# Twenty weight slots in place of seventeen, fp32 expert bias and a new order of the works in a transformer layer on one core

## The chip, the cores and the metric

The kernel runs on 1 core of a Trainium2 chip, as one launch. The metric is the device time of that core in microseconds (us), the median of 3 runs. All tensors are fp32 in HBM; there is one execution per run.

## The reference, cut to what matters

One layer over 256 latent tokens (d_model 1024) and 256 context tokens: a mixer of two attention branches (8 heads of GQA and 8 heads of MLA), then a mixture of 32 experts, of which each token takes 4. Both are modulated by rows of an `ada` projection of the conditioning vector: shift, scale and gate, `g1` for the mixer, `g2` for the experts.

```
h  = rms_norm(x)*(1 + scale1) + shift1 ; hc the same for the context
y  = sig(gate_a) * (gqa(h, hc) @ w_o_gqa) + sig(gate_b) * (mla(h, hc) @ w_o_mla)
x  = x + g1 * (y @ w_out)
h2 = rms_norm(x)*(1 + scale2) + shift2
p  = softmax-gated top 4 of 32 of (h2 @ router)
x  = x + g2 * sum_e p_e * (swiglu_clamped(h2 @ w1[e] + b1[e]) @ w2[e] + b2[e])
```

`w1` has 32 x 1024 x 2048 elements and `w2` 32 x 1024 x 1024: 12 MB for each expert, 384 MB in all. Everything before the experts reads about 80 MB.

## The kernel before, in words

**Two parts.** Up to some 407 us of the profiled execution lies the mixer, with the router at its end; then come the 32 experts. Every weight is read once, whether or not many tokens use it.

**The mixer** is cut into works, each a generator that gives up control after a few instructions: `T` (tokens transposed), `r, c, f, h, l, k` (first projection), `q, g` (queries, gates), `p, a, b` (MLA), `S, P, V` (scores, probabilities, values of 16 heads), `wa, wb` (branch projections, two chunks of 512 columns each), `o` (output projection, `out_chunk`), `rest` (the 16 later rows of `ada`, `ada_rest`, each a matmul group at L249 and then columns at L260 or a broadcast at L269), `bi` (preparation of the expert bias, `bias1`) and `x` (the residual read again). The string `PLAN` lists the works in the order in which their steps are issued; `needs` has what must be finished first. Dense products are made at near fp32 accuracy as three matmuls of split operands (L145 to L147), whose weights are split on ACT (L110) and on POOL or DVE (L112).

**Expert weights** come as 1 MB loads, 8 of `w1` (L968) and 4 of `w2` (L1002) for each expert, into a ring of 17 slots in SBUF (`RING`, `wx`). Most slots hold other things during the mixer: keys and values of attention (`e`, `m`), gates (`g`), the merged branches (`y`), or the streaming buffer `w` of the mixer's own weights; `n0` to `n3` lie in memory that all the mixer's pools give back at its end. A load can be issued as soon as its slot's last reader is done.

**What sets the order.** All loads of weights are issued by SyncE (SP), in order: a load that waits for its slot holds back all that follow it. For the experts, `keep_order` fixes each engine's order as written. In the mixer a scheduler places the loads by where the program's text has them.

**One expert**: up to 64 tokens. `gather` (L925 ff., once for each pair of experts) builds a one-hot matrix on DVE (L932), scaled on POOL (L934), gathers with 16 matmuls (L940) and evicts (L946, L948). `up` starts its two banks with the bias (4 bf16 matmuls at L964, from a three-way bf16 split of `b1` in 96 rows) and adds 32 matmuls (L972). `swiglu` is a chain on DVE and ACT; `turned` transposes (L163) and copies (L994); `down` has 16 matmuls (L1007) and an eviction (L1013); `scatter` (L1022, L1023), for each pair, adds into the residual, and writes the output (L1025) after the last. Between `up` and `turned` of an expert, steps of a scatter or a gather stand on PE. The last expert has none there. `b2` is loaded and added by `bias2` in the third expert.

Of the kernel before, what the change touches and what calls it, by code (L numbers as in the profile page):

```python
# [24 lines left out]
T0*3 l0 T0 f0 f1 h0 h1 T0 k0 f2 r1 l1 h2 c1 k1 f3 k2 c2 T1 h3 r5 f4 k3 T1 bi h4 tab T0 f5 r4 bi T1 l4 c0 r2 bi  # L25
T1 r0 f6 l3 r3 T1 l2 k4 k5 h6 T1 r7 c3 f7 k6 k7 end q0 bi T1 bi q0 l5 q0 T0 c7 l6 kv*2 h7 ss bi c5 kv*2 q0 bi
r6 q0 kv bi q0 q1 h5 kv mp q1 bi q0 q1 bi q0 bi q1 mp bi l7 q0 c6 q0 q1 q0 q1 end g0 q1*3 g0*2 bi g0 q1 c4
g0*4 g1 q1 g1 g0 g1 S0 g1 S2 g1*2 P0 S0 g1 g2 rest*2 P1 g2 g1 mp V0 rest*2 g1 g2*2 S2 g2 S4 g2 S3 g2*3 rest g3
rest S1 g3 rest P2 S3 S4 V2 S1 g3*2 rest g2 P3 g3*2 V3 g3 a0 g3 P4 rest S5*2 rest a0 V4 a0 rest g3 rest*3 a0
# [5 lines left out]
wb1 rest o0*4 wb1*2 o0 o1 o0*2 rest wb1 o0 o1*8 x o1*3
"""
SLOTS = ("e0", "e1", "e2", "e3", "m0", "m1", "g0", "g1", "y0", "y1")

RING = ("e0", "e1", "e2", "e3", "m0", "m1", "g0") + ("w",) * NW + ("y0", "y1", "n0", "n1", "n2", "n3", "g1")
# [9 lines left out]
class Layer:  # L49
# [174 lines left out]
    def silu(self):  # L224
# [6 lines left out]
        self.cs = self.k2([128, 8, 32], "cs")  # L231
# [3 lines left out]
        self.bsc = self.k2([128, 2, 8], "bsc")  # L235
# [476 lines left out]
    def ada_rest(self):  # L712
        nc, I = self.nc, self.I
# [14 lines left out]
        last(15, ev)  # L728

    def out_chunk(self, c):  # L730
# [38 lines left out]
    def mixer(self):  # L769
# [7 lines left out]
        def gates(c):  # L777
            if c // 2 not in self.ga:
# [40 lines left out]
    def route(self):  # L819
# [9 lines left out]
        self.xn = self.q([128, 2, D], "xn", 1)  # L829
# [54 lines left out]
    def bias1(self):  # L884

        nc = self.nc
        v = nc.vector
# [3 lines left out]
        f = f.rearrange("p h c -> p (h c)")  # L891
        self.b1 = self.k([96, 2 * D], "b1", BF)
        self.sel = self.k([96, NE], "bsel", BF)
        v.tensor_copy(self.sel, self.ck[:96, K_E32:K_E32 + NE])
        for c in range(4):
            cs = slice(c * 512, (c + 1) * 512)
            v.tensor_copy(self.b1[:, cs], f[:, cs])
            yield
            for lo in (32, 64):
                r = slice(lo, lo + 32)  # L900
# [24 lines left out]
    def gather(self, e0):  # L925

        nc = self.nc
        xg = self.xg = self.q([128, 8, 2, 64], "xg")
        oh, og = self.a([128, 2, 2, 64]), self.a([128, 2, 2, 64])
        sh = [128, 2, 64]  # L930
        for t in range(2):
            nc.vector.tensor_tensor(oh[:, t], self.ck[:, K_I64:K_I64 + 64].unsqueeze(1).broadcast_to(sh),  # L932
                                    self.rp[:, t, e0:e0 + 2].unsqueeze(2).broadcast_to(sh), op=OP.is_equal)
            nc.gpsimd.tensor_tensor(og[:, t], oh[:, t], self.gm[:, t, e0:e0 + 2].unsqueeze(2).broadcast_to(sh), op=OP.mult)  # L934
        yield
        for kk in range(8):
# [12 lines left out]
            yield
        b = self.bank("x", [128, T])  # L950
# [6 lines left out]
    def up(self, e, xg):  # L957
# [276 lines left out]
```

## Time and profile before

| | |
|---|---|
| median of 3 runs | 1351.97 us (the two near it 1351.41 and 1351.97; one far off, 3543.51) |
| the profiled execution | 1351.25 us, of which its span is 1349.5 us |
| PE busy in the span | 1217.8 us (90%), mean granted clock 0.971 |
| DVE, ACT, POOL busy | 457.3, 288.8, 162.8 us |
| HBM read, written | 465.82 MB, 1.05 MB; mean 346 GB/s |
| chain that ended last | PE 51%, DMA 37%, DVE 8% |

The slices of the profile read in two halves. In the first 12 of 40 slices (up to about 405 us) the moved bytes swing between 32 and 348 GB/s, while PE is at 0.6 to 0.9; in all later ones but the last, 399 to 422 GB/s are moved and the DMA engines are at 0.9 or above. Clock figures are shares of full speed; a slice at 0.5 would be the lower of two levels throughout.

### The profile page before, as it was taken

How to read it: one execution, taken by the hardware profiler on the slowest of the kernel's cores; microseconds unless marked ns; L12 is line 12 of the kernel's file. 1: busy time of each engine (PE TensorE's matmuls, PEld its weight loads, DVE VectorE, ACT ScalarE, POOL GpSimd, SP SyncE). 2: the span in 40 equal slices, each digit the busy share in tenths (PEclk: the TensorE clock that was granted, in tenths of full speed). 3: DMA queues.
4: the chain of work that ended last, by engine and by line, in shares of the span. 5: the costliest groups of instructions: out<-in, count | busy, mean ns of one | idle time of the engine just before them, and what ended most of it. 6: DMA issues, size and time to landing. Idle time of an engine off the chain costs nothing.

```text
span 1349.5 us, 15322 instructions
## 1 busy us (share of the span) xinstructions
PE 1217.8 (90%) x6031; PEld 605.2 (45%) x6031; DVE 457.3 (34%) x968; ACT 288.8 (21%) x626; POOL 162.8 (12%) x181
## 2 busy tenths in 40 slices
PE   6979999899988999999999989889898898989896
PEld 5667775667863333433344332333333242433331
DVE  5777447785341132221221211212121112212112
ACT  3356666666430001100010000100000000100000
POOL 2645421233520000000000000000000000000000
PEclk9989999999989989999999999999999999999998
DMA  8614646403879999999999999999999999999994
GB/s 348 238 62 182 228 140 222 145 32 126 327 306 399 408 413 421 421 422 421 421 420 421 421 421 421 421 422 420 422 421 422 421 421 421 422 421 420 422 422 188
DMA packets 67227, 467.91 MB, mean 347 GB/s; under 512 B 7632, under 2 KB 7760, under 8 KB 11760
## 3 DMA queue, kind: packets, MB, share of 16 engines
q1 hardware_dynamic: 67152, 466.89, 85.2%
q8 instruction: 49, 0.80, 0.2%
q14 instruction: 26, 0.21, 0.0%
HBM read 465.82 MB, written 1.05 MB: 346 GB/s over the span
## 4 chain that ended last, share of the span: by engine, by line
PE 51%; DMA 37%; DVE 8%; ACT 2%; issue 1%; POOL 1%; SPq 0%; DVEq 0%; ACTq 0%; POOLq 0%
PE bs L972 15%; PE bx L1007 9%; DMA e<-in_w_dram 9%; DMA n<-in_w_dram 7%; DMA w<-in_w_dram 6%; DMA g<-in_w_dram 5%; DMA m<-in_w_dram 4%; DMA y<-in_w_dram 4%; PE bacc L145 3%; PE bacc L147 3%; PE bacc L146 3%; PE bacc L940 2%; PE bx L163 2%; PE bt L940 2%; PE bx L249 2%; PE bt L163 1%
## 5 line engine op out<-in xcount | busy, mean ns | idle before, releaser
L981 ACT ACTIVATE a<-a 128x512 f32<-128x512 f32 x32 | 20.1, 629 | 716.5 <-DVE a L980 716.5
L980 DVE TENSOR_SCALAR a<-bs 128x512 f32<-128x512 f32 x32 | 22.1, 692 | 435.2 <-PE bs L972 435.2
L972 PE MATMUL bs<-e,xg 128*64 128x512 f32 x504 | 114.8, 596 | 8.1 <-DMA e<-in_w_dram 8.1
L112 POOL TENSOR_TENSOR wl<-w,wh 128x512 fp32r<-128x512 f32 (+1 forms) x81 | 105.3, 1309 | 126.2 <-ACT wh L110 106.9
L934 POOL TENSOR_TENSOR c<-c,gm 128x128 f32<-128x128 f32 x32 | 12.1, 399 | 870.6 <-DVE c L932 854.8
L972 PE MATMUL bs<-n,xg 128*64 128x512 f32 x472 | 108.0, 596 | 9.7 <-DMA n<-in_w_dram 9.7
L1013 DVE TENSOR_TENSOR y<-bx,g 64x512 f32<-64x512 f32 x64 | 44.0, 688 | 207.3 <-PE bx L1007 206.6
L972 PE MATMUL bs<-w,xg 128*64 128x512 f32 x360 | 82.8, 596 | 6.8 <-DMA w<-in_w_dram 6.8
L940 PE MATMUL bacc<-c,xn 128*128 128x128 f32 x256 | 42.9, 337 | 38.6 <-DVE c L932 37.8
L110 ACT CAST wh<-w 128x512 fp32r<-128x512 f32 (+1 forms) x108 | 65.2, 612 | 42.4 <-PE bacc L147 32.8
L972 PEld LDWEIGHTS bs<-e,xg 128*64 128x64 f32 x504 | 34.8, 136 | 82.1 <-issue 58.9
L972 PEld LDWEIGHTS bs<-n,xg 128*64 128x64 f32 x472 | 32.5, 136 | 79.7 <-issue 56.9
L940 PEld LDWEIGHTS bacc<-c,xn 128*128 128x128 f32 x256 | 39.3, 242 | 51.9 <-DVE c L932 51.0
L972 PE MATMUL bs<-m,xg 128*64 128x512 f32 x248 | 57.0, 595 | 3.8 <-DMA m<-in_w_dram 3.8
L972 PE MATMUL bs<-g,xg 128*64 128x512 f32 x240 | 57.1, 596 | 3.8 <-DMA g<-in_w_dram 3.8
L972 PE MATMUL bs<-y,xg 128*64 128x512 f32 x224 | 52.1, 597 | 4.8 <-DMA y<-in_w_dram 4.8
L1007 PE MATMUL bx<-n,a 128*64 128x512 f32 x232 | 54.1, 611 | 0.0
L1007 PE MATMUL bx<-e,a 128*64 128x512 f32 x232 | 52.3, 595 | 0.0
L972 PEld LDWEIGHTS bs<-w,xg 128*64 128x64 f32 x360 | 24.9, 136 | 59.8 <-issue 44.4
L946 DVE TENSOR_SCALAR xg<-bt,A,B 128x128 f32<-128x128 f32 x64 | 21.9, 405 | 79.7 <-PE bt L940 74.3
L1007 PE MATMUL bx<-w,a 128*64 128x512 f32 x192 | 46.2, 626 | 0.7 <-ACT a L994 0.7
L948 ACT ACTIVATE xg<-bacc,B,A 128x128 f32<-128x128 f32 x64 | 24.1, 456 | 73.2 <-PE bacc L940 73.2
(351 smaller groups left out, 1966.6 us busy)
## 6 DMA issues: line engine op xcount, KB each, us to landing
e<-in_w_dram SPq DMA_DIRECT2D x92, 1024.0 KB, 19.8
n<-in_w_dram SPq DMA_DIRECT2D x88, 1024.0 KB, 19.8
w<-in_w_dram SPq DMA_DIRECT2D x69, 1024.0 KB, 19.8
m<-in_w_dram SPq DMA_DIRECT2D x46, 1024.0 KB, 19.8
g<-in_w_dram SPq DMA_DIRECT2D x45, 1024.0 KB, 19.8
y<-in_w_dram SPq DMA_DIRECT2D x44, 1024.0 KB, 19.8
w<-in_ada_dram SPq DMA_DIRECT2D x24, 1024.0 KB, 5.6
w<-in_wga_dram SPq DMA_DIRECT2D x8, 1024.0 KB, 4.8
```

The source lines that it names most:

```text
L110: self.nc.scalar.copy(h, src)
L112: eng.tensor_sub(l, src, h.bitcast(F32))
L145: mm(o, lh, rh, start=start, stop=False, **kw)
L146: mm(o, lh, rl, start=False, stop=False, **kw)
L147: mm(o, ll, rh, start=False, stop=stop, **kw)
L163: self.nc.tensor.transpose(o, i, self.ident)
L249: nc.tensor.matmul(b[j:j + 32, :256], self.cs[:, kk], u[:, kk], start=kk < 4, stop=kk >= 4, tile_position=(0, j))
L940: nc.tensor.matmul(b[:, kk % 4], self.xn[:, t, kk * 128:(kk + 1) * 128], oh[:, t], start=t == 0, stop=t == 1)
L948: nc.scalar.activation(xg[:, k], b[:, i], AF.Identity, bias=c, scale=a)
L972: mm(b[64 * j:64 * j + 64], xg[:, k, e % 2], w[:, lo:lo + 512], start=False, stop=k == 7, tile_position=(0, 64 * j))
L1007: nc.tensor.matmul(b[64 * j:64 * j + 64], lh, w[:, i, j * 512:(j + 1) * 512], start=f == 0, stop=f == 7, tile_position=(0, 64 * j))
L1013: nc.vector.tensor_mul(y[r:r + 64, cs], b[q], self.g2[q, cs])
```

## The change

- **Slots.** `RING` has 20 slots: `z0`, `z1` and `r0` are new. Pools are laid out anew: `ws` and a new pool `r` stand on the right side, `x2T` goes through work tiles, `xg` and `y` have one buffer each, and the attention's own pools (`h`, `k2`) are closed when the last values are done (`after_attention`), so `n0` to `n3` exist before the mixer ends. `dynamic_dma_scratch_size=1024` makes a scratch area in SBUF smaller.
- **Early loads.** Three new works issue 14 expert loads from the plan: `EZ` (2, into `z0, z1`), `EA` (after `V15`: 8, into `e` and `n`), `EG` (after `wb1`: 4, into `m` and `g`). The other 6 of the ring (`w` three times, `y0, y1, r0`) follow as before.
- **Expert bias.** `bias1` with its bf16 split is gone. `biases` loads `b1` (two halves of 32 rows) and `b2` into one fp32 tile; `up` starts with 4 plain fp32 matmuls over 32 rows. `b2` is no longer loaded among the experts.
- **Works.** `rest` keeps 12 rows of `ada`; the 4 of `g2` are the work `late`, placed near the mixer's end. `PLAN` is another order throughout.
- **Gather** evicts in quarters, and makes the scaled one-hot and its transposes after the matmuls; those of the first gather stand behind `up(0)`.
- **The end.** The scatter of the last pair is made in two parts of 64 rows: that of expert 30 between `up(31)` and `turned`, that of expert 31 at the end.

```diff
-RING = ("e0", ..., "m0", "m1", "g0") + ("w",) * NW + ("y0", "y1", "n0", "n1", "n2", "n3", "g1")
+LATER = ("n0", "n1", "n2", "n3")
+RING = ("z0", "z1", "e0", "e1", "e2", "e3") + LATER + ("m0", "m1", "g0", "g1") + ("w",) * NW + ("y0", "y1", "r0")
...
+    def expert_part(self):
+        e, i = divmod(self.nx, 12)
+        src = self.I["w1"][e, i * 128:i * 128 + 128] if i < 8 else self.I["w2"][e, i * 256 - 2048:i * 256 - 1792]
+        w = self.wx([128, 2 * D] if i < 8 else [128, 2, D])
+        self.nc.sync.dma_start(w, src if i < 8 else src.rearrange("(p j) d -> p j d", j=2))
+        return w
+    def weights(self):
+        return self.ahead.pop(0) if self.ahead else self.expert_part()
+    def after_attention(self):
+        self.attention.close()
+        self.open(self.ctx, "q", 1)
+        for slot in LATER:
+            self.q([128, 2, D], slot, 1)
+        self.q([128, D], "xg", 1)
+        yield from self.ahead_of_time(8)
...
-    def ada_rest(self):
+    def ada_rest(self, lo, hi):
...
-        for i in range(16):
+        for i in range(lo, hi):
...
+        w = self.works = {..., "rest": self.ada_rest(0, 12), "late": self.ada_rest(12, 16), ...}
+        need = {..., "late": ["rest"], "EA": ["EZ", "V15"], "EG": ["EA", "wb1"]}
+        w.update(EZ=self.ahead_of_time(2), EA=self.after_attention(), EG=self.ahead_of_time(4))
...
-    def bias1(self):
-        f = self.s("x", [96, 2, D])
-        for j in range(3):
-            nc.sync.dma_start(f[32 * j:32 * j + 32], self.I["b1"].rearrange("e (h c) -> e h c", h=2))
-        ...
-        for c in range(4):
-            v.tensor_copy(self.b1[:, cs], f[:, cs])
-            for lo in (32, 64):
-                for part in range(lo // 32):
-                    v.tensor_sub(f[r, cs], f[r, cs], self.b1[r, cs])
-                    v.tensor_copy(self.b1[r, cs], f[r, cs])
+    def biases(self):
+        self.b12 = self.k([128, D], "b12")
+        for j in range(2):
+            nc.sync.dma_start(self.b12[64 + 32 * j:96 + 32 * j], self.I["b1"][:, j * D:j * D + D])
+        nc.sync.dma_start(self.b12[0:NE], self.I["b2"])
...
     def up(self, e, xg):
-                mm(b[64 * j:64 * j + 64], self.sel[:, e:e + 1].broadcast_to([96, 64]), self.b1[:, lo:lo + 512],
-                   start=True, stop=False, tile_position=(0, 64 * j))
+                r = slice(64 + 32 * n, 96 + 32 * n)
+                mm(b[64 * j:64 * j + 64], self.ck[r, K_E32 + e:K_E32 + e + 1].broadcast_to([32, 64]),
+                   self.b12[r, j * 512:j * 512 + 512], start=True, stop=False, tile_position=(64 + 32 * n, 64 * j))
-            w = self.wx([128, 2 * D])
-            nc.sync.dma_start(w, self.I["w1"][e, k * 128:(k + 1) * 128])
+            w = self.weights()
...
-    def scatter(self, G, y, last):
+    def scatter(self, G, y, last, r=slice(0, 128)):
-                nc.tensor.matmul(b, G[:, t * 128:(t + 1) * 128], y[:, cs], start=True, stop=True)
+                nc.tensor.matmul(b, G[r, t * 128:(t + 1) * 128], y[r, cs], start=True, stop=True)
...
     def experts(self):
-                side = self.gather(e + 1) if e + 1 < NE else iter(())
+                side = self.scatter(self.G, y, False, slice(0, 64))
...
-        for _ in self.scatter(*shown, True):
+        for _ in self.scatter(self.G, y, True, slice(64, 128)):
```

(The plan itself, of which one line would tell nothing, is shown by the orders below.)

**SP around the last branch projection.** Each row is one load; `wob` and `wout` are the mixer's last weights, `in_w` is an expert's, and the letter before the arrow is the slot. Before:

```order
L450 DMA w_3539<-in_wob_dram 128x2048
L760 DMA x_3675<-in_x_dram 128x1024 x2
L450 DMA w_3576<-in_wob_dram 128x2048
L450 DMA w_3633<-in_wob_dram 128x2048
L450 DMA w_3700<-in_wob_dram 128x2048
L968 DMA e_988_4117<-in_w_dram 128x2048
L968 DMA e_989_4123<-in_w_dram 128x2048
L450 DMA w_3776<-in_wout_dram 128x2048
L968 DMA e_990_4129<-in_w_dram 128x2048
L450 DMA w_3806<-in_wout_dram 128x2048
L968 DMA e_991_4135<-in_w_dram 128x2048
L450 DMA w_3862<-in_wout_dram 128x2048
```

And now, the same place, up to the last `wob` and the first `wout`:

```order
L477 DMA w_3510<-in_wob_dram 128x2048
L104 DMA e_851_3474<-in_w_dram 128x2048
L477 DMA w_3570<-in_wob_dram 128x2048
L104 DMA e_843_3453<-in_w_dram 128x2048
L104 DMA e_852_3476<-in_w_dram 128x2048
L104 DMA n_853_3478<-in_w_dram 128x2048
L104 DMA n_854_3480<-in_w_dram 128x2048
L104 DMA e_842_3451<-in_w_dram 128x2048
L104 DMA n_855_3482<-in_w_dram 128x2048
L104 DMA n_869_3565<-in_w_dram 128x2048
L477 DMA w_3637<-in_wob_dram 128x2048
L477 DMA w_3713<-in_wout_dram 128x2048
```

These follow it on the same queue, up to the last two loads of `ada`:

```order
L272 DMA w_3743<-in_ada_dram 128x2048
L477 DMA w_3756<-in_wout_dram 128x2048
L104 DMA m_937_3829<-in_w_dram 128x2048
L477 DMA w_3806<-in_wout_dram 128x2048
L272 DMA w_3816<-in_ada_dram 128x2048
L104 DMA m_938_3831<-in_w_dram 128x2048
L104 DMA g_939_3833<-in_w_dram 128x2048
L104 DMA g_943_3854<-in_w_dram 128x2048
L477 DMA w_3899<-in_wout_dram 128x2048
L272 DMA w_3921<-in_ada_dram 128x2048
L272 DMA w_3951<-in_ada_dram 128x2048
```

Eight expert loads of this stretch now stand ahead of the last `wob`, and four more ahead of the last `wout` and the last two `ada` loads; before, none stood ahead of a `wob`, and five ahead of the last `wout` (two rows behind the last one shown).

**DVE near the end of the first projection.** `x_523` is the fp32 bias, `b_136` its bf16 parts; L299 makes a modulated token block and L141 its low part, for which PE waits. Before:

```order
L299 TENSOR_SCALAR c_684<-m_26_104,A_30_114,B_31_115 128x256
L902 TENSOR_TENSOR x_523<-x_523,b_136_527 32x512 x2
L903 CAST b_136_527<-x_523 32x512 x2
L897 CAST b_136_527<-x_523 96x512
L902 TENSOR_TENSOR x_523<-x_523,b_136_527 32x512 x2
L141 TENSOR_TENSOR c_687<-c_684,c_686 128x256
L903 CAST b_136_527<-x_523 32x512 x2
L112 TENSOR_TENSOR wl_715<-h_174_692,wh_714 128x512
L902 TENSOR_TENSOR x_523<-x_523,b_136_527 32x512
L262 TENSOR_SCALAR B_31_115<-bx_705,cols_89 128x2
L263 TENSOR_SCALAR A_30_114<-bx_705,bsc_111,cols_89 128x2
L903 CAST b_136_527<-x_523 32x512
```

And now, where L326 is what L299 was, and L168 what L141 was:

```order
L326 TENSOR_SCALAR c_630<-e_27_105,A_32_116,B_33_117 128x256
L168 TENSOR_TENSOR e_35_119<-c_630,e_34_118 128x256
L326 TENSOR_SCALAR c_663<-m_28_106,A_32_116,B_33_117 128x256
L168 TENSOR_TENSOR c_666<-c_663,c_665 128x256
L326 TENSOR_SCALAR c_693<-m_28_106,A_32_116,B_33_117 128x256
L289 TENSOR_SCALAR B_33_117<-bx_699,cols_91 128x2
L168 TENSOR_TENSOR c_696<-c_693,c_695 128x256
L290 TENSOR_SCALAR A_32_116<-bx_699,bsc_113,cols_91 128x2
L139 TENSOR_TENSOR wl_709<-h_169_650,wh_708 128x512
L326 TENSOR_SCALAR c_712<-e_27_105,A_32_116,B_33_117 128x256
L326 TENSOR_SCALAR c_740<-m_28_106,A_32_116,B_33_117 128x256
```

The subtractions and casts of the bias stood between the modulations; none is left.

**PE at the end of the program.** `w` of the last `up` (L972 before, L984 now), the transposes of `turned` (L163, L190), `down` (L1007, L1018) and the scatter (L1022, L1033). Before:

```order
L972 MATMUL bs_7880<-m_1807_7928,xg_7699 64x512 x2
L972 MATMUL bs_7881<-m_1807_7928,xg_7699 64x512 x2
L163 MATMUL bx_7942<-ck_90,a_7936 128x128 x4
L1007 MATMUL bx_7949<-g_1814_7950,a_7947 64x512 x4
L1007 MATMUL bx_7949<-w_7956,a_7947 64x512 x4
L1007 MATMUL bx_7949<-w_7962,a_7947 64x512 x4
L1007 MATMUL bx_7949<-w_7968,a_7947 64x512 x4
L1022 MATMUL bacc_7976<-y_7833,c_7742 128x512
L1022 MATMUL bacc_7980<-y_7833,c_7742 128x512
L1022 MATMUL bt_7984<-y_7833,c_7742 128x512
L1022 MATMUL bt_7988<-y_7833,c_7742 128x512
```

And now:

```order
L984 MATMUL bs_7892<-r_1847_7940,xg_7709 64x512 x2
L984 MATMUL bs_7893<-r_1847_7940,xg_7709 64x512 x2
L1033 MATMUL bacc_7954<-y_7845,c_7754 128x512
L1033 MATMUL bacc_7957<-y_7845,c_7754 128x512
L1033 MATMUL bt_7960<-y_7845,c_7754 128x512
L1033 MATMUL bt_7963<-y_7845,c_7754 128x512
L190 MATMUL bx_7966<-ck_92,a_7948 128x128 x4
L1018 MATMUL bx_7973<-z_1858_7974,a_7971 64x512 x4
L1018 MATMUL bx_7973<-z_1859_7980,a_7971 64x512 x4
L1018 MATMUL bx_7973<-e_1860_7986,a_7971 64x512 x4
L1018 MATMUL bx_7973<-e_1861_7992,a_7971 64x512 x4
L1033 MATMUL bacc_8000<-y_7845,c_7754 128x512
```

Four scatter matmuls stand between `up` and `turned` now; the four at the end, of which the last row here is the first, stay as many as before.

## Rows read from the trace of the kernel before

**Rows 1.** Windows: stretch, its us; PE, PEld, DVE, ACT, POOL busy; clock, DMA, GB/s.

```profile
46.00:75.00 29.00, 23.70 (x133) 17.99 (x132) 27.40 (x52) 7.32 (x18) 18.31 (x30) 0.93 0.42 158
75.00:87.00 12.00, 12.00 (x51) 9.70 (x50) 4.95 (x10) 10.19 (x29) 8.96 (x9) 0.89 0.26 88
180.00:293.00 113.00, 100.61 (x618) 68.87 (x617) 80.72 (x222) 72.91 (x175) 23.84 (x23) 0.95 0.42 147
293.00:390.00 97.00, 96.51 (x481) 76.17 (x480) 48.56 (x92) 49.67 (x94) 43.85 (x34) 1.00 0.57 216
390.00:407.00 17.00, 10.73 (x70) 9.69 (x70) 9.29 (x40) 5.34 (x13) 0.76 (x2) 0.70 0.95 388
440.00:800.00 360.00, 339.91 (x1618) 138.82 (x1616) 85.44 (x151) 28.48 (x61) 5.29 (x14) 0.97 1.01 419
1325.00:1330.00 5.00, 2.58 (x8) 1.15 (x10) 1.41 (x3) 0.58 (x1) 0.00 (x0) 0.70 0.59 244
1330.00:1340.00 10.00, 9.21 (x33) 2.90 (x30) 1.38 (x2) 0.00 (x0) 0.00 (x0) 0.81 0.04 16
```

**Rows 2.** Chain in the experts, 440 to 800: start us, us, engine, tile, line.

```profile
549.66 13.76 PE bs L972 x64
...
593.18 1.91 PE bacc L1022 x4
595.10 0.86 PE bt L1022 x2
...
604.73 13.76 PE bs L972 x64
```

**Rows 3.** Chain at the end, 1310 to 1350.

```profile
1302.50 19.80 DMA m<-in_w_dram
...
1322.35 1.96 PE bs L972 x8
...
1326.69 1.00 PE bx L163 x4
...
1328.41 9.76 PE bx L1007 x32
```

**Rows 4.** Timeline of SP's queue, 300 to 412: start us, us, line, load.

```profile
395.04 0.33 SPq L968 DMA_DIRECT2D g<-in_w_dram  x1
408.81 2.04 SPq L968 DMA_DIRECT2D e<-in_w_dram  x2
```

**Rows 5.** Timeline of PE, 389 to 412: start us, busy us, line, operation, [idle before].

```profile
389.82 0.40 PE L147 MATMUL bacc<-wh,y 128*128 128x512 f32 x1
...
398.78 0.19 PE L847 MATMUL bx<-maskb,ub 128*128 128x32 bf16 x1 [3.77 <-DVE maskb L844]
...
399.84 3.75 PE L940 MATMUL bacc<-c,xn 128*128 128x128 f32 x16 [0.77 <-DVE g L862]
...
406.12 0.38 PE L163 MATMUL bx<-ck,c 128*128 128x128 f32 x2
406.43 0.63 PE L964 MATMUL bs<-b,bsel 96*64 96x512 bf16 x4
406.88 5.32 PE L972 MATMUL bs<-e,xg 128*64 128x512 f32 x24
```

**Rows 6.** Chain from 46 to 75 us, shares by line.

```profile
by line: DVE x L902 28.0%; DVE b L903 21.5%; issue 7.1%; DVE c L299 6.4%; DVE b L897 5.9%; DVE wl L112 4.9%; DVE e L141 4.5%; DVE c L141 3.2%; ACT c L140 2.6%; PE bs L147 2.4%; DVE B L262 2.2%; DVE A L263 2.0%; PE bt L145 1.7%; PE bt L146 1
```

**Rows 7.** Timeline of PE, 222 to 240: one row of `ada` and its broadcast.

```profile
229.23 1.07 PE L249 MATMUL bx<-w,cs 128*32 128x256 f32 x16
230.23 0.70 PE L269 MATMUL bx<-c,ck 128*128 128x256 f32 x2
```

**Rows 8.** DMA issues of the page: line, engine, count, KB each, us to landing.

```profile
e<-in_w_dram SPq DMA_DIRECT2D x92, 1024.0 KB, 19.8
```

**Rows 9.** DMA issues from 290 to 412 us.

```profile
w<-in_wob_dram SPq DMA_DIRECT2D x4, 1024.0 KB, 4.9
w<-in_wout_dram SPq DMA_DIRECT2D x4, 1024.0 KB, 6.4
```

More of the change, by code (lines that the diff above doesn't have):

```diff
@@ L24 @@
 PLAN = """
[L25 to L29, printed above, removed]
@@ L35 @@
[L35 to L39 removed]
+bi T0*2 l0 f0 f1 h0 T0 h1 T0 k0 f2 r1 l1 h2 r0 k1 f3 k2 c2 T1 h3 r5 f4 k3 T1 h4 tab f5 r4 l4 c0 T1 r2 T0*2
+T1*2 r3 T1 l2 f6 l3 EZ k4 r7 k5 h6 f7 k6 c1 k7 end q0 T1 q0 c5 kv*2 l5 q0 T0 c7 l6 h7 ss c3 EZ*2 kv q0 r6 q0
+kv q0 kv q1 h5 q1 kv q0 q1*3 g0 l7 q0 q1 q0 c6 q0 q1*2 g0 q0 end q1 g0*2 q1 g1 q1 c4 g0*4 g1 mp g0 g1 mp S0 g1
@@ L61, in open @@
         kw.setdefault("reuse_waits", "tile")
+        if name in ("ws", "r"):
+            kw["side"] = "right"
         self.pools[name] = ctx.enter_context(self.tc.tile_pool(name=f"{name}{self.n}", bufs=bufs, **kw))
@@ L93, in wx, with ahead_of_time @@
             return self.w(shape, dt)
-        return self.tile("q" if slot[0] == "n" else "s", shape, dt, slot, 1)
+        return self.tile({"n": "q", "r": "r"}.get(slot[0], "s"), shape, dt, slot, 1)
+    def expert_part(self):
[6 more added lines that the diff above has]
+        return self.ahead.pop(0) if self.ahead else self.expert_part()
+    def ahead_of_time(self, n):
+        for _ in range(n):
+            self.ahead.append(self.expert_part())
+            yield
+    def after_attention(self):
[5 more added lines that the diff above has]
+        yield from self.ahead_of_time(8)
     def k(self, shape, tag, dt=F32):
@@ L727, in ada_rest @@
             ev = new
-        last(15, ev)
+        last(hi - 1, ev)
     def out_chunk(self, c):
@@ L748, in out_chunk @@
                 self.transpose(b[:, j], self.x[:, t, c * 512 + j * 128:c * 512 + (j + 1) * 128])
-            nc.vector.tensor_mul(self.x2T[:, ks, ts], b, self.A2[:, ks, 0:1].broadcast_to([128, 4, 128]))
-            for k in range(4 * c, 4 * c + 4):
-                nc.tensor.matmul(self.logits[:, t], self.x2T[:, k, ts], self.rw[:, k], start=k == 0 and t == 0, stop=k == 7,
+            x2T = self.a([128, 4, 128])
+            nc.vector.tensor_mul(x2T, b, self.A2[:, ks, 0:1].broadcast_to([128, 4, 128]))
+            for j in range(4):
+                k = 4 * c + j
+                nc.tensor.matmul(self.logits[:, t], x2T[:, j], self.rw[:, k], start=k == 0 and t == 0, stop=k == 7,
                                  skip_group_check=True)
@@ L919, in bias2 @@
                 b = self.bank("acc")
-                nc.tensor.matmul(b, gT[:, t * 128:(t + 1) * 128], b2[:, cs], start=True, stop=True)
+                nc.tensor.matmul(b, gT[:, t * 128:(t + 1) * 128], self.b12[0:NE, cs], start=True, stop=True)
                 z = self.a([128, 512])
@@ L1031, in experts @@
         first = len(self.nc.cur_bb.bb.instructions)
-        for _ in self.gather(0):
-            pass
-        side, shown = iter(()), None
+        gather = self.gather(0)
+        for _ in range(9):
+            next(gather)
+        shown = None
         for e in range(NE):
-            xg = self.xg
-            act = self.swiglu(*self.up(e, xg), 512)
+            act = self.swiglu(*self.up(e, self.xg), 512)
             if e % 2 == 0:
-                side = self.scatter(*shown, False) if shown else iter(())
-                y = self.q([128, D], "y")
+                side = self.scatter(*shown, False) if shown else gather
+                y = self.tile("r", [128, D], F32, "y", 1)
+            elif e + 1 < NE:
                 shown = self.G, y
+                side = self.gather(e + 1)
             else:
-                side = self.gather(e + 1) if e + 1 < NE else iter(())
+                side = self.scatter(self.G, y, False, slice(0, 64))
             for _ in range(7 if e % 2 else 3):
@@ L1081, in overflow @@
             v.memset(one, 1.0)
-            h2 = [self.q([128, 4, T], "xg") for _ in range(2)]
+            h2 = [self.q([128, 4, T], "xg", 1), self.tile("r", [128, 4, T], F32, "y", 1)]
             self.normed_T(h2)
-            ge = self.k([128, 2], "goe")
+            ge = self.q([128, 2], "goe", 1)
             with tc.For_i(0, NE, 1) as i:
@@ L1142, in build @@
     def build(self):
-        self.loaded, self.nsplit, self.nx = {}, 0, 0
+        self.loaded, self.ahead, self.nsplit, self.nx = {}, [], 0, 0
         self.open(self.ctx, "w", 1)
@@ L1147, in build @@
             self.s(slot, [128, 2, D])
+        self.attention = ExitStack()
         with ExitStack() as pre:
-            for p in ("h", "k2", "ws"):
-                self.open(pre, p, 1)
+            self.open(pre, "ws", 1)
+            for p in ("k2", "h"):
+                self.open(self.attention, p, 1)
             self.setup()
```

81 lines of the change are left out of this document (35 added, 46 removed).

## The prediction

> **What bounds the kernel now.** I read the stages first [rows 1]. There are two limits. Among the experts (440 to 800 us is typical) the DMA share is 1.01 and 419 GB/s are moved, so a 1 MB load (1.0486 million bytes) costs 2.50 us; eight are in flight, and 8 x 2.50 is the 19.80 us of one load's latency [rows 8]. PE is the quicker there: two experts start 604.73 − 549.66 = 55.07 us apart while loads are still ahead of it [rows 2], or 27.5 us for one, against 12 x 2.50 = 30.0 us for an expert's loads. So the experts end by DMA, and the chain at the end shows it: a load of 19.80 us, issued at 1302.50, releases the last matmuls of `up` at 1322.35 [rows 3].
>
> The mixer is another matter. In 293 to 390 PE is busy 96.51 of 97 us: PE is the limit, and DMA has room (0.57). In 46 to 75 PE is busy only 23.70 of 29 us while DVE is at 27.40, and the shares of the chain there name the bias split: L902 28.0%, L903 21.5%, L897 5.9% [rows 6].
>
> The join: the last output matmul starts at 389.82, PE then waits for the router, and `up(0)` starts at 406.88 [rows 5]. The first load into a used slot is issued 1.93 us later, at 408.81 [rows 4]. By then 17 of 384 loads are done or under way. The last `w1` load is the 380th; so 363 loads and `b2` take 408.81 to 1322.35 = 913.5 us, 2.52 each. From 1322.35 to the end of the span are 27.15 us. The time is therefore **start of `up(0)` + 1.93 + loads left x 2.50 + tail**, and each part of the change is priced by which of these it moves. The sum is made against the profiled execution, 1351.25 us (span 1349.5 and 1.75 around it), which is 0.7 us below the median of the runs.
>
> **The change, part by part.**
>
> *Bias split removed.* 28 DVE instructions leave the chain. Its share, 55.4% of 29 = 16.1 us, is the most that can come back [rows 6]; none comes back if other DVE or ACT work ends the same waits. I take what PE loses there: 29 − 23.70 = 5.3 us idle, 0.07 x 29 = 2.0 us of clock, and 0.11 x 12 = 1.3 us of clock in the 12 us behind it [rows 1]: **−8.6**, between 0 and −16.1. The change's order on DVE has nothing in their place, so no new wait is due there.
>
> *Four rows of `ada` moved to the end.* A row with its broadcast takes 1.0 us (229.23 to 230.23) and half of 0.70 [rows 7]: 1.35 us, 5.4 for four. They go where PE has no idle time [rows 1], so all of it counts: +5.4. They leave a stretch in which PE is busy 100.61 of 113 us, so 0.89 of it comes back: −4.8 (0 if they filled waits, −5.4 if not). Net **+0.6**, between 0 and +5.4.
>
> *SP's queue.* Eight expert loads now stand ahead of the last `wob` and twelve ahead of the last `wout`; before, none and five. The mixer's loads landed in 4.9 and 6.4 us with the DMA about half used [rows 9]. With an expert load under way, each mixer load lands up to 2.50 later. Most were issued well ahead of their use, so I take **+1.5**, between 0 and +4; the larger loss is a rival.
>
> *Start of `up(0)`.* Four bf16 matmuls (0.45 us from 406.43 to 406.88) become four fp32 ones; a matmul of `up` takes 13.76/64 x 2 = 0.43 [rows 2], so 1.7 us in a row. The transposes of the gather go behind `up(0)` (0.3 us, 406.12 to 406.43 [rows 5]). Net **+1.0**, between 0 (two row tiles at once) and +1.3. The quarter evictions I cost at nothing: they run beside the 16 gather matmuls.
>
> *Three more slots.* 360 loads in place of 363 remain behind `up(0)`, if all 20 have landed: **−7.5**, between 0 and −7.5. That they do: of the six that come last, `y0, y1, r0` must follow the last output matmul, and between it and `up(0)` lie 17.06 us [rows 5], room for 6.8 loads of 2.50. *`b2`* (128 KB, an eighth of a load) leaves the stream: **−0.3**.
>
> *Each expert.* The bias adds 1.3 us to PE's 27.5: 28.8, still below 30.0, so it costs nothing while loads set the pace; the cover is 1.2 us an expert, and each us beyond costs 32. Single buffers of `xg` and `y` are read before they are written again in PE's order, and cost nothing under the same cover.
>
> *The end.* Four scatter matmuls go into the gap that PE has between 1324.31 and 1326.69. By an earlier scatter (1.91 and twice 0.86 [rows 2]) they take 3.6 us, the gap is 2.4: +1.2. Behind the gap the clock falls to 0.70 and 0.81 [rows 1], and `down` takes 9.76 us [rows 3]; 0.30 x 5 + 0.19 x 10 = 3.4 us are lost to the lower level. Whether a filled gap keeps it up no row shows; half is −1.7. Net **−0.5**, between +1.2 and −2.2.
>
> The Trainium skill ("TensorE: Matmul & The Clock Gate", "HAM oscillation") says that idle gaps between bursts of matmuls put TensorE back to its low clock. By that all 3.4 us would return, and the sum would be 1.7 lower.
>
> *The new order of the rest.* Works of equal content change places; no row prices that. In 180 to 293 PE loses 12.4 us idle and 0.05 x 113 = 5.7 of clock [rows 1], 18 in all; both the gain and a loss of that kind are possible. I take **0**, ±6 within the forecast.
>
> Sum: −8.6 + 0.6 + 1.5 + 1.0 − 7.5 − 0.3 − 0.5 = −13.8, or **1337.5 us**.
>
> **Rivals.**
> 1. *The order recovers the 180 to 293 stretch too.* For: the removed DVE work, four `ada` rows less, and nothing else is the limit there (DVE 80.72, ACT 72.91 of 113). Against: its waits are short chains between engines, and only their order is new. All 18: 1319.5. Chance 0.19.
> 2. *Slower: the loads hold up SP.* In the order now, an `e` and two `n` loads stand directly ahead of the last `wob`, and one of them waits until keys or values of the last heads are read; all behind it wait with it. PE would then stand idle in the stretch that has no slack now. Price: nine mixer loads (the last `wob`, four `wout`, four `ada`), each late by one expert load of 2.50: 22.5 us, 1360. It decides once these stalls exceed the 13.8 of the gain. For: the stretch is PE's entirely. Against: five `e` and `m` loads already stood among the `wout` loads, without a gap on PE. Chance 0.12.
> 3. *The slots bring nothing*, because the last of them land after `up(0)`, or the router's end comes earlier and PE, not DMA, gains: 1337.5 + 7.5 = 1345. For: before, loads were issued up to 395.04, 12 us ahead of `up(0)` [rows 4], and DMA was at 0.95 in the stretch [rows 1]. Against: the count of 6.8 above. Chance 0.14.
> 4. *PE becomes the limit among the experts.* 32-row tiles now alternate with 128-row ones. Around L249, whose tiles have 32 columns, no pause shows (it ends and L269 starts, 230.23), so I give it 0.03. Were 1.2 us of cover exceeded by 0.8, 32 x 0.8 = 26 us: 1363. The Trainium skill ("TensorEngine Tiling (Array Packing)", "Key Properties") says that changing the tiling mode drains the engine; it gives no time.
>
> My forecast, within some 8 us of 1337.5, has 0.52.
>
> **Numbers.** Predicted 1337.5. The range takes in the order's gain and the third case, and just misses the slowest: 1316 to 1358. About 2% is what a measurement here can tell from no change: below 1325 is faster, above 1379 slower. Faster: most of rival 1 and little of the forecast, 0.19. Slower: only rivals 2 and 4 at more than their price, 0.03. The same: 0.78.
>
> **What would show it.** Right: no bias split on DVE in 46 to 75 and PE above 0.9 of it; `up(0)` at about 401; the first reuse 2 us behind it with 20 loads landed; loads still at 419 GB/s with PE waiting at each; a tail of about 27 us with its clock a little higher. Wrong: PE idle before the last branch or output matmuls with a DMA as its releaser (rival 2); PE without waits for loads among the experts (rival 4); DMA busy through to `up(0)` (rival 3); a clock and PE share near 1 from 180 on (rival 1).

## The result and the profile after

The change takes 1328.36 us (median of 4 runs, 1325.94 to 1330.45), the kernel before beside it 1351.69: ratio **0.9831, 95% interval 0.9807 to 0.9855**. It is faster, by 23 us, 1.7%: inside the range, within the 2% that the prediction counts as the same, and 9 us below the predicted 1337.5. The profiled executions (1351.25 and 1327.47) are cut at the points of the prediction's sum:

| | before | after | change | forecast |
|---|---|---|---|---|
| last output matmul starts | 389.82 | 374.30 | −15.5 | −6.5 |
| from there to `up(0)` | 17.06 | 18.09 | +1.0 | +1.0 |
| `up(0)` to the first reuse of a slot | 1.93 | 1.98 | 0 | 0 |
| first reuse to the last `w1` matmul | 913.5 | 905.7 | −7.9 | −7.8 |
| from there to the end of the span | 27.15 | 25.65 | −1.5 | −0.5 |
| sum | | | −23.8 | −13.8 |

So the surprise lies in the mixer. In the rows of the changed kernel L172 to L174 are the split products (L145 to L147 before), L276 a row of `ada`, L952 the gather, L977 the bias, L984 `up`, L190 the transposes, L1018 `down` and L1033 the scatter. Its windows (columns as in [rows 1]):

```profile
46.00:75.00 29.00, 29.00 (x175) 23.93 (x174) 15.24 (x33) 13.19 (x30) 18.27 (x33) 1.00 0.59 234
180.00:293.00 113.00, 104.31 (x603) 75.32 (x604) 88.45 (x247) 79.97 (x189) 31.32 (x28) 0.95 0.36 129
293.00:380.00 87.00, 85.74 (x475) 65.44 (x474) 38.08 (x73) 39.10 (x76) 33.39 (x26) 1.00 0.78 311
380.00:400.00 20.00, 15.51 (x81) 9.53 (x82) 6.59 (x32) 5.64 (x11) 0.76 (x2) 0.74 0.49 199
440.00:800.00 360.00, 343.80 (x1658) 132.15 (x1659) 83.44 (x145) 26.90 (x57) 4.54 (x12) 0.99 1.01 419
```

From 46 to 75 PE is busy throughout at the full clock, as forecast; in 180 to 293 it is busy 3.7 us longer than [rows 1] showed, at the same clock of 0.95, so 3.7 of the 18 us lost there came back. Among the experts the rate is the old 419 GB/s. From 380 to 400 the DMA idles half of the time, since all slots are full. SP's queue shows it:

```profile
319.18 0.33 SPq L104 DMA_DIRECT2D e<-in_w_dram  x1
319.56 0.90 SPq L104 DMA_DIRECT2D n<-in_w_dram  x2
320.57 0.65 SPq L477 DMA_DIRECT2D w<-in_wob_dram  x1
...
375.98 0.43 SPq L104 DMA_DIRECT2D r<-in_w_dram  x1
394.37 2.04 SPq L104 DMA_DIRECT2D z<-in_w_dram  x2
```

What SP waited for in 300 to 400 us (us in total, times, longest):

```profile
SPq L104 <- PE bx L174: 17.2, 2, 9.8
```

This is rival 2's place: an `e` load waited up to 9.8 us for the values of a head, until 319.18, and the last `wob` behind it was issued at 320.57. But PE has no gap from 320 to 374. The last load of the 20 is issued at 375.98, 16 us ahead of `up(0)`. PE there, against [rows 5]:

```profile
374.30 0.39 PE L174 MATMUL bacc<-wh,y 128*128 128x512 f32 x1
...
383.73 0.18 PE L875 MATMUL bx<-maskb,ub 128*128 128x32 bf16 x1 [3.77 <-DVE maskb L872]
...
391.38 1.09 PE L977 MATMUL bs<-b,ck 32*64 32x512 f32 x8
392.39 3.65 PE L984 MATMUL bs<-z,xg 128*64 128x512 f32 x16
```

The four fp32 bias matmuls (x8 in the trace) take 1.01 us where 0.45 stood, up to the start of `up`. The chain at the end, against [rows 3]:

```profile
1280.19 19.82 DMA r<-in_w_dram
...
1300.05 1.94 PE bs L984 x8
1301.99 1.91 PE bacc L1033 x4
1303.90 1.72 PE bt L1033 x4
1305.62 0.69 PE bx L190 x4
...
1307.02 7.11 PE bx L1018 x32
```

The scatter fills the gap behind `up`, and `down` takes 7.11 us where it took 9.76.

### The profile page after: what moved, and what is told of

It reads as the page before. It is cut to its first block, busy times and chain, and to the rows that moved or that the text cites. A ratio compares the mean times of both kernels' runs of the same rounds, so it can differ in the third digit from the quotient of the medians.

```text
span 1325.7 us, 15561 instructions
## 1 busy us (share of the span) xinstructions
PE 1226.0 (92%) x6167; PEld 602.0 (45%) x6167; DVE 443.2 (33%) x943; ACT 289.9 (22%) x626; POOL 157.7 (12%) x181
## 4 chain that ended last, share of the span: by engine, by line
PE 52%; DMA 39%; DVE 5%; ACT 1%; issue 1%; POOL 0%; SPq 0%; DVEq 0%; ACTq 0%; POOLq 0%
PE bs L984 14%; DMA r<-in_w_dram 9%; PE bx L1018 8%; DMA m<-in_w_dram 8%; DMA w<-in_w_dram 8%; DMA e<-in_w_dram 8%; DMA n<-in_w_dram 7%; PE bacc L172 3%; PE bacc L174 3%; PE bacc L173 3%; PE bx L276 2%; PE bx L190 2%; PE bt L190 2%; PE bacc L952 2%; PE bs L172 1%; PE bt L952 1%
## 5 line engine op out<-in xcount | busy, mean ns | idle before, releaser
L984 PE MATMUL bs<-e,xg 128*64 128x512 f32 x416 | 93.7, 595 | 2.6 <-DMA e<-in_w_dram 2.6
L984 PE MATMUL bs<-n,xg 128*64 128x512 f32 x400 | 90.9, 596 | 3.9 <-DMA n<-in_w_dram 3.9
L984 PE MATMUL bs<-w,xg 128*64 128x512 f32 x312 | 72.2, 597 | 5.1 <-DMA w<-in_w_dram 5.1
L952 PE MATMUL bacc<-c,xn 128*128 128x128 f32 x256 | 41.1, 326 | 38.5 <-DVE c L945 37.8
L952 PEld LDWEIGHTS bacc<-c,xn 128*128 128x128 f32 x256 | 37.4, 232 | 51.8 <-DVE c L945 51.0
L984 PEld LDWEIGHTS bs<-e,xg 128*64 128x64 f32 x416 | 28.9, 137 | 65.0 <-issue 55.2
L984 PEld LDWEIGHTS bs<-n,xg 128*64 128x64 f32 x400 | 27.6, 137 | 65.0 <-issue 55.4
L984 PE MATMUL bs<-g,xg 128*64 128x512 f32 x208 | 47.7, 597 | 2.2 <-DMA g<-in_w_dram 2.2
L984 PE MATMUL bs<-y,xg 128*64 128x512 f32 x208 | 47.4, 594 | 2.2 <-DMA y<-in_w_dram 2.2
L984 PE MATMUL bs<-z,xg 128*64 128x512 f32 x208 | 47.5, 596 | 1.0 <-DMA z<-in_w_dram 1.0
L1018 PE MATMUL bx<-n,a 128*64 128x512 f32 x208 | 47.2, 595 | 0.7 <-ACT a L1006 0.7
L1018 PE MATMUL bx<-e,a 128*64 128x512 f32 x208 | 47.1, 595 | 0.0
L984 PEld LDWEIGHTS bs<-w,xg 128*64 128x64 f32 x312 | 21.1, 136 | 54.1 <-issue 40.1
L984 PE MATMUL bs<-m,xg 128*64 128x512 f32 x192 | 43.7, 594 | 1.4 <-DMA m<-in_w_dram 1.4
L952 PE MATMUL bt<-c,xn 128*128 128x128 f32 x256 | 37.8, 297 | 0.0
L952 PEld LDWEIGHTS bt<-c,xn 128*128 128x128 f32 x256 | 35.8, 217 | 0.0
## 6 DMA issues: line engine op xcount, KB each, us to landing
e<-in_w_dram SPq DMA_DIRECT2D x78, 1024.0 KB, 19.8
n<-in_w_dram SPq DMA_DIRECT2D x76, 1024.0 KB, 19.8
w<-in_w_dram SPq DMA_DIRECT2D x57, 1024.0 KB, 19.8
z<-in_w_dram SPq DMA_DIRECT2D x40, 1024.0 KB, 19.8
m<-in_w_dram SPq DMA_DIRECT2D x38, 1024.0 KB, 19.8
g<-in_w_dram SPq DMA_DIRECT2D x38, 1024.0 KB, 19.8
y<-in_w_dram SPq DMA_DIRECT2D x38, 1024.0 KB, 19.8
```

The costliest lines, as they stand in the source:

```text
L952: nc.tensor.matmul(b[:, kk % 2], self.xn[:, t, kk * 128:(kk + 1) * 128], oh[:, t], start=t == 0, stop=t == 1)
L984: mm(b[64 * j:64 * j + 64], xg[:, k, e % 2], w[:, lo:lo + 512], start=False, stop=k == 7, tile_position=(0, 64 * j))
L1018: nc.tensor.matmul(b[64 * j:64 * j + 64], lh, w[:, i, j * 512:(j + 1) * 512], start=f == 0, stop=f == 7, tile_position=(0, 64 * j))
```

## The experiments

Medians, ratio to the kernel before with its interval, and where the slots start in SBUF by the memory plan of each program (bytes past a multiple of 512; `r0` lies at 480 where the others lie at 384), which came to matter. x4 and x5 have one run each, 1327.9 and 1326.8 us, and stand apart below:

| kernel | us | ratio | slots start at | GB/s, 900 to 1200 us |
|---|---|---|---|---|
| before | 1351 to 1352 | 1 | 320 | 421 |
| the change | 1328.4 | 0.983 | 384 | 421 |
| x1, bias alone | 1336.3 | 0.989 [0.9872, 0.9908] | 256 | 427 |
| x2, bias and order | 1327.4 | 0.9825 [0.9807, 0.9843] | 256 | 427 |
| x9, bias and late rows | 1340.4 | 0.9914 [0.9898, 0.9931] | 256 | 427 |
| x3, 17 slots | 1336.6 | 0.9895 [0.988, 0.991] | 384 | 421 |
| x6, no late rows | 1324.9 | 0.9799 [0.9778, 0.982] | 384 | 421 |
| x7, early loads last | 1332.2 | 0.9848 [0.9832, 0.9865] | 384 | 421 |
| y0, before, shifted | 1339.2 | 0.9914 [0.9899, 0.9928] | 0 | 427 |
| y1, bias alone, shifted | 1345.4 | 0.9964 [0.9952, 0.9977] | 320 | 421 |
| y2, the change, aligned | 1317.8 | 0.9758 [0.9739, 0.9777] | 0 | 427 |
| y3, y2 with `b2` later | 1311.7 | 0.971 [0.9696, 0.9723] | 0 | 427 |

**x1, x2: the mixer.** In the kernel before, `bias1` and the matmuls of `up` as in the change; for x2 also the new `PLAN` (without `EZ`, `EA`, `EG`) and `ada_rest` in two works.

```diff
-    def bias1(self): ...   # 28 DVE instructions, three loads
+        self.b12 = self.k([128, D], "b12")
+        for j in range(2):
+            nc.sync.dma_start(self.b12[64 + 32 * j:96 + 32 * j], self.I["b1"][:, j * D:j * D + D])
```

> The kernel before with the expert bias alone changed: two fp32 loads of b1, no bf16 split on DVE, four plain fp32 bias matmuls per expert; 17 slots and the old order of works stay. Theory A (two causes of like size in the mixer: the split held PE up by about 8.6 us, the new order brings another 7 to 8): up(0) starts at 406.9 - 8.6 + 1.0 = 399.3 us, the time is 1351.3 - 7.6 = 1343.7, and PE loses as much in 180 to 293 us as before. Rival B (the split's whole share of its chain, 16 us, came back and the order brought nothing): up(0) at about 392, time about 1336.5. Rival C (other DVE work ends the same waits): up(0) at 407, time 1352.

> The kernel of x1 with the new order of works too, the ada rows of g2 placed late as in the change, but none of its early-load works: 17 slots, the old pools, b2 loaded among the experts, the old end. Theory A: up(0) at 406.9 - 8.6 - 7 + 1.0 = 392.3 us, time 1351.3 - 14.5 = 1336.8, that is 7 below x1. Rival B: no gain over x1, wherever that stands. Rival D (the mixer's gain comes from the pools of its own and the early expert loads, not from the order): up(0) as in x1, 399, time 1343.7, and the missing 7 us in 180 to 293.

By time alone rival B holds for x1 (1336.3). By landmarks it doesn't: `up(0)` starts at 401.23, not 392. And x2 was as fast as the change with three slots fewer, which the sum had no room for. Part of what both gained lay behind `up(0)`: 363 loads in 906.1 (x1) and 904.3 us (x2), 2.50 and 2.49 each, against 913.5 before and 2.52 in the change. In 900 to 1200 us their loads ran at 427 GB/s. With the bias selector gone (64 bytes), all their slots start 64 bytes lower than before.

PE up to the last output matmul, in the kernel before, in x1, in x2 and in the change:

```profile
0.00:389.82 389.82, 354.37 (x1991) 266.07 (x1992) 242.47 (x571) 215.98 (x473) 150.75 (x149) 0.97 0.52 189
0.00:383.56 383.56, 353.88 (x1992) 266.38 (x1992) 225.35 (x542) 215.97 (x473) 145.79 (x149) 0.98 0.52 191
0.00:377.92 377.92, 353.52 (x1988) 267.91 (x1988) 222.81 (x540) 216.34 (x473) 145.61 (x149) 0.97 0.52 191
0.00:374.30 374.30, 350.01 (x1987) 264.75 (x1988) 223.95 (x540) 216.13 (x473) 145.62 (x149) 0.98 0.57 212
```

PE idles 35.5, 29.7, 24.4 and 24.3 us of it: the bias gave back 5.8 us of idle time, the new order another 5.3. As for rival D, `up(0)` of x2 starts at 395.66, 5.6 us ahead of x1's and 3.3 behind the change's. Profiles of the same mixer differ by as much (x1 401.23 and y1 398.13; y2 392.87 and y3 389.26), so it stays open whether the early loads and the new pools have a part in these 3.3 us.

**y0, y1, y2: where the slots start.** One unused tile each, ahead of the slots:

```diff
+        self.k([128, 48], "pad")    # y0, in the kernel before: 192 bytes
+        self.k([128, 16], "pad")    # y1, in x1: 64 bytes
+        self.k([128, 32], "pad")    # y2, in the change: 128 bytes, and 480 at the end of the pool "r"
         self.open(self.ctx, "w", 1)
```

> The kernel before with 192 unused bytes per partition ahead of the slots and nothing else: every slot then starts at a multiple of 512 bytes in SBUF, where it started at 320 past one. Theory H (the loads among the experts ran at 426.5 GB/s in x1 and x2 and at 421 elsewhere because their slots start at a multiple of 256 bytes): 426.5 GB/s, 363 loads of 2.46 in place of 2.49 us, some 11 us less behind up(0), time 1351.3 - 11 = 1340; up(0) at 407 as before. Rival G (the rate hung on what the bias change did to the queue or to PE, its b1 loads or its bias matmuls): 421 GB/s and 1351.

> The kernel of x1 with 64 unused bytes per partition ahead of the slots, so that they start where those of the kernel before did (320 past a multiple of 512). Theory H: 421 GB/s again, up(0) at 401 as in x1, time 1336.3 + 11 = 1347, so that the bias alone is worth 4 to 6 us of its 15. Rival G: 426.5 GB/s and 1336.

> The changed kernel with 128 unused bytes ahead of the slots on the left and 480 in the pool on the right, so that all 20 slots start at a multiple of 512 bytes (they started at 384 past one, r0 at 480). Theory H: 426.5 GB/s among the experts, 360 loads of 2.46, some 11 us less, up(0) at 392.4, time 1328 - 11 = 1317, faster than all so far. Rival G: 421 GB/s and 1328.

Theory H three times over: −12, +9 and −11 us, with nothing changed but addresses. The same window of y0 and of y1:

```profile
900.00:1200.00 300.00, 269.59 (x1259) 105.54 (x1260) 64.86 (x115) 21.62 (x46) 4.53 (x12) 0.98 1.01 427
```
```profile
900.00:1200.00 300.00, 273.43 (x1290) 102.67 (x1290) 62.32 (x111) 21.28 (x45) 3.78 (x10) 0.98 1.01 421
```

The DMA share is 1.01 in both: the engines are as busy and move 1.4% less. The change itself stands at 384, slow as before; alignment had no part in its gain. With it taken out, the bias alone is worth 1351.1 − 1345.4 = 5.7 us at the old addresses (y1), and 1339.2 − 1336.3 = 2.9 at multiples of 256 bytes (x1 against y0, whose intervals meet). x2 against x1 (same addresses) gives the order 8.9, the late rows with it. With the 8.2 us of the slots (x3, below), 5.7 + 8.9 + 8.2 = 22.8 of the 23.3 us are accounted for.

**x9: one piece of the order.** x1 with the four `ada` rows of `g2` late, in the old order otherwise.

```diff
-    ... "rest": self.ada_rest(), ...     # 16 rows
+    ... "rest": self.ada_rest(0, 12), "late": self.ada_rest(12, 16), ...   # late among the steps of o0 and o1
```

> The kernel of x1 (fp32 bias, 17 slots, old order) with one piece of the new order: the four ada rows of g2 become a work of their own and stand among the output projection; all other works stay in the old order. Its slots start at a multiple of 256 bytes, as in x1 and x2. Theory K (the 9 us between x1 and x2 come from these rows leaving 180 to 250 us, where PE waited around them for their loads and evictions, about 5.8 us in x1 against 2 in x2): time within 3 us of x2, 1325 to 1330. Rival L (they come from the new order of the attention works): time within 3 us of x1, 1334 to 1339. Half of each would lie at 1332.

Neither: 4 us slower than x1, though the two intervals still meet, and `up(0)` at 405.63, 4.4 us later. The rows cost their time at the end and left holes where they had stood. The stretch from 180 to 290 us in x1, in x9 and in x2:

```profile
180.00:290.00 110.00, 97.62 (x601) 66.82 (x601) 81.84 (x230) 71.34 (x172) 21.95 (x21) 0.95 0.39 138
```
```profile
180.00:290.00 110.00, 94.26 (x535) 67.52 (x534) 83.53 (x231) 71.55 (x170) 21.70 (x22) 0.91 0.31 110
```
```profile
180.00:290.00 110.00, 101.30 (x577) 73.17 (x577) 85.09 (x240) 77.34 (x183) 30.14 (x27) 0.92 0.34 120
```

Without the rows PE is busy 3.4 us less there in x9. In x2 other work fills the holes, and PE is 7 us busier than in x9. So the rest of the new plan, the attention works and all others together, is worth 1340.4 − 1327.4 = 13 us, and the late rows take 4 of it back. Where in the mixer the order gains is less sure: in this stretch x2 idles 3.7 us less than x1, but the clock is 0.92 in place of 0.95, another 3.3 us.

**x6, x3, x7: late rows, slots, early loads**, each in the change.

```diff
-"late": self.ada_rest(12, 16)
+"late": iter(())                                   # x6
-RING = ("z0", "z1", "e0", ... "y0", "y1", "r0")
+RING = ("e0", ... "y0", "y1")                      # x3, and EZ issues none
-... V13 EA S15 EA ... late EG*2 ... V14 EA ...
+... late*2 x b3 o1 EA*9 EG*5                       # x7
```

> The changed kernel without the four late rows of ada: their loads, matmuls, evictions and the addition into g2 are left out, so g2 is only its bias. Theory A (PE is the limit where they stand, so all of their 1.35 us each counts): up(0) 5.4 us earlier, at 387.0, time 1322.1. Rival F (they fill waits of PE at the mixer's end): up(0) less than 2 us earlier, time 1325.5 or above.

> The changed kernel with 17 slots: z0, z1 and r0 taken out of the ring, all else as in the change. Theory A (each slot is one load of 2.50 us less behind up(0)): up(0) at 392.4 as in the change, last w1 matmul 7.5 us later, time 1327.5 + 7.5 = 1335.0. Rival E (the three loads only fill DMA time that PE's pace or the idle DMA ahead of up(0) gives back): no difference, 1327.5.

> The changed kernel with the 12 early expert loads of EA and EG written behind the whole mixer in the plan (EZ stays); the scheduler still moves them forward, so that on SP one wob load and two wout loads stand ahead of expert loads that they stood behind. Theory N (where the text places them hardly matters, since slots free at the same times and DMA has room): up(0) within 1 us of 392.4, time 1328.4 within 2. Rival O (early placing is worth as much as slots): some loads land behind up(0), time 1333 or more. Rival P (expert loads held the mixer's loads up): up(0) 2 us or more earlier, time 1326 or less.

x6: `up(0)` at 390.44, 2 us earlier; 3.5 us of time, nearer to rival F than to 5.4, with an interval that meets that of the change. x3: theory A, 8.2 us for three slots (914.7 us from `up(0)` to the last `w1` matmul, 907.7 in the change). x7 is unclear: 1332.2, but its interval meets that of the change. `up(0)` was 1.2 us later. The rest of its profile's loss lies in 440 to 520 us, x7 first, then the change:

```profile
440.00:520.00 80.00, 76.60 (x347) 30.88 (x348) 21.14 (x37) 6.16 (x13) 0.76 (x2) 0.92 0.96 386
```
```profile
440.00:520.00 80.00, 76.39 (x358) 27.99 (x359) 20.31 (x35) 5.28 (x12) 0.76 (x2) 0.98 1.00 410
```

PE is as busy in both, at a lower clock in x7, and the loads run slower: here, right behind `up(0)`, PE hands out the slots and sets the pace (y3, below). Whether the placing caused the lower clock stays open.

**x4, x5: the end**, in the change, one run each.

```diff
-                side = self.scatter(self.G, y, False, slice(0, 64))
+                side = iter(())                    # x4
+                side = self.filler(y)              # x5: 4 matmuls of that size, no additions
```

> The changed kernel with the last scatter made whole at the end, as before: nothing stands between up(31) and turned. Theory Q (an idle gap there can drop TensorE's clock for the matmuls of down): down starts 5.8 to 6.1 us behind the last w1 matmul and takes from 6.5 to 9.2 us by the state of the clock, longer than 6.5 in four of five; the tail from the last w1 matmul is 24 to 27 us. Rival R (the clock there has nothing to do with the gap): 6.5 us, as in the changed kernel.

> As x4, but with four matmuls of the same size in the gap whose result nobody reads, without their additions on DVE. Theory Q: down starts 7.0 us behind the last w1 matmul and takes 6.5 us at the full clock; the tail is about 25.6 us. Rival S (it was the additions, or the scatter's split, that helped): down takes as long as in x4.

PE in x4, then in x5:

```profile
1304.80 0.71 PE L190 MATMUL bx<-ck,a 128*128 128x128 f32 x4 [2.41 <-DVE a L996]
1306.24 5.28 PE L1018 MATMUL bx<-z,a 128*64 128x512 f32 x16 [0.73 <-ACT a L1006]
1311.36 3.60 PE L1018 MATMUL bx<-e,a 128*64 128x512 f32 x16
```
```profile
1301.37 1.98 PE L1045 MATMUL bacc<-y,c 64*128 64x512 f32 x4
1303.19 1.88 PE L1045 MATMUL bt<-y,c 64*128 64x512 f32 x4
1305.00 0.74 PE L190 MATMUL bx<-ck,a 128*128 128x128 f32 x4
1306.47 3.65 PE L1018 MATMUL bx<-z,a 128*64 128x512 f32 x16 [0.73 <-ACT a L1006]
```

Theory Q: behind matmuls that nobody reads the first half of `down` (x16 in the trace) takes 3.65 us, where it took 5.28 behind the gap, and the clock from 1306 to 1312 us is 1.00 in x5 against 0.72 in x4. Over all profiles, from its first matmul's start to its last's, `down` took 6.50 us in all seven kernels with a filled gap, and in the seven with an empty one 6.50 once (y1) and 7.86 to 9.16 six times: the empty gap costs the clock most times, not always. The tail was 25.1 us on average filled and 25.7 empty: the 1.2 us that the fill adds eat most of it.

**y3: the pace behind `up(0)`.** y2 with one number changed.

```diff
-            if e == 2:
+            if e == 16:
                 self.bias2()
```

> The kernel y2 (the change with all slots at multiples of 512 bytes) with the addition of b2 moved from the third expert to the seventeenth. Theory T (right behind up(0) PE sets the pace: in 440 to 520 us of y2 the loads ran at 393, 370, 395 and 407 GB/s in place of 426, 6.6 us lost, and the b2 matmuls, 5.7 us, are in it; later PE waits for loads and hides them): 425 GB/s or near in 440 to 520, time 1317.8 - 5 = 1313. Rival U (those losses come from the low clock and the gathers there, or the work costs the same where it goes): 1318.

Theory T: 6.1 us less, intervals apart, the fastest kernel here. y2, then y3:

```profile
440.00:480.00 40.00, 39.12 (x163) 14.78 (x163) 13.51 (x23) 2.87 (x6) 0.00 (x0) 0.90 0.93 382
480.00:520.00 40.00, 37.48 (x192) 15.72 (x190) 7.38 (x14) 3.09 (x7) 0.76 (x2) 0.96 0.98 401
```
```profile
440.00:480.00 40.00, 40.00 (x186) 13.24 (x184) 8.00 (x12) 1.22 (x2) 0.00 (x0) 1.00 1.01 413
480.00:520.00 40.00, 37.48 (x190) 15.29 (x185) 10.22 (x19) 4.09 (x9) 0.76 (x2) 1.00 1.01 427
```

The loads lost 6.6 us against 427 GB/s in y2 and 1.3 in y3. The clock rose with it: in y2 it is 0.64 from 470 to 475.5 us, where the `b2` matmuls run, and 0.69 from there to 480, and in y3 1.00 throughout 440 to 520. How much of the 6.1 us is the work and how much the clock that fell with it, so much of rival U, no run here separates.

## Why the prediction was right in kind and short in size

- **The sum and its three limits held**: start of `up(0)`, loads, tail. Three terms came out nearly to the number. Three slots, −7.5 forecast, are 8.2 us in x3. The end, −0.5 forecast, is −0.6 between the mean tails, partly by luck: half of 3.4 us was taken because no row showed whether a filled gap keeps the clock up; it did in seven of seven, but behind an empty gap `down` took only 1.7 us longer on average. The step from the router to `up(0)` came out at +1.0 by luck too: the bias matmuls cost 0.56 of the forecast 1.3, moving the transposes gave nothing back (6.59 us from the first gather matmul to the first of the bias in both kernels), and 0.47 arose where nothing was forecast, ahead of the first mask matmul (9.43 us behind the last output matmul in place of 8.96).
- **The step that failed is "The new order of the rest ... I take 0, ±6".** x2 against x1 gives −8.9, and −13 when the late rows that came with it are set apart (x9). The prediction named the 18 us that PE loses in 180 to 293 and gave their recovery a chance of 0.19, as all or nothing. What came was no half of rival 1 either: that stretch gave back 3.7 us of the 18, and the order took 5.3 us off PE's idle time over the whole mixer. This term alone makes up the 9 us between 1337.5 and 1328.4, because the smaller misses nearly cancel: SP's queue and the slots came out 1.5 and 0.7 better, the bias 1.9 worse.
- **Late `ada` rows**: net +0.6 forecast; +4.1 in x9, between the bounds 0 and +5.4 (PE idled 34.1 us up to the last output matmul there, 29.7 in x1). The row's own time counts where PE is the limit, and leaving a stretch full of waits gives nothing back unless the order is made anew. In the change they cost 3.5 (x6), and `up(0)` 2.0.
- **Bias split**: −8.6 + 1.0 forecast, 5.7 us of time (y1), 2.9 at the other addresses. PE did get all of 46 to 75 us back, and `up(0)` was 5.65 us early in x1 and 8.75 in y1. But the prediction costed the fp32 matmuls of each expert at nothing under the cover of the loads, and there is no such cover in the first experts: in 440 to 520 us y1 moved 394 GB/s at a clock of 0.91, the kernel before 412 at 0.96 (rows below). By its 121st expert load (649.41 us against 654.72) 5.3 of the 8.75 were left, and in x1 against y0 3.3 of 6.15.
- **SP's queue**: +1.5 forecast; no gap on PE shows it. Rival 2 happened on SP (the `wob` at 320.57 behind an `e` load) and cost nothing, since `wob` came before its use. Rivals 3 and 4 didn't occur as written, but rival 4's limit, PE, does hold in 440 to 520 us, in the first experts (y2 and y3).

The stretch from 440 to 520 us in y1, then in the kernel before:

```profile
440.00:520.00 80.00, 74.11 (x338) 32.00 (x338) 22.15 (x40) 7.34 (x16) 1.51 (x4) 0.91 0.97 394
```
```profile
440.00:520.00 80.00, 74.08 (x352) 30.13 (x350) 22.75 (x41) 7.20 (x16) 1.51 (x4) 0.96 1.01 412
```

How much of that is the bias and how much the clock, no run here separates.

## What to carry to other kernels

Compare two kernels by landmarks before comparing their times: x1's 15 us looked like the whole bias chain, and 9 to 12 of them were the addresses. Landmarks of single profiles scatter too, here by up to 3.6 us for one mixer, so a difference of that size needs the medians of several runs. An order's value can be bounded from the idle time of the engine that it feeds: it can gain (x2) as well as lose (x9), and a term of zero was the largest miss here. Cover is local: a stage that is bound by loads on average can be bound by an engine at its start, and work that must go somewhere in it goes late.

## What the runs showed of the hardware

Loads of 1 MB into SBUF (128 rows of 8 KB) ran at 427 GB/s when every slot started at a multiple of 256 bytes (0 or 256 past one of 512; six kernels) and at 421 when most or all started at 64 or 128 past one (320 and 384; the eight others). One load's latency with eight under way was 19.6 us in y2 and 19.8 in the change. Shifting the slots alone moved the time by 9 to 12 us of 1340.

The Trainium skill ("DMA: Bandwidth & Descriptors", "How a descriptor splits into AXI transactions") says that a descriptor which does not start at a multiple of 256 bytes begins with a transaction at the 256-byte boundary below, and that the bytes before its start are fetched unused and still cost. By that page an 8 KB row takes 33 transactions in place of 32, an estimate of up to 3%. The direction agrees with y0, y1 and y2; the measured 1.4%, the same for 64 and 128 bytes, settles the size. The page speaks of reads, while the address shifted here is the one written; that its rule is the cause no run here shows.
